# An encoder trunk on one core: waits for single input tiles, banded attention ahead of its gates, and another order of the output stages

## The chip, the cores and the metric

The kernel runs on one core of one Trainium2 chip. The metric is the device time of one execution in microseconds (us), as the median of several runs. Five engines matter: TensorE (PE; the loading of its stationary operand is listed as PEld), VectorE (DVE), ScalarE (ACT), GpSimd (POOL) and SyncE (SP). SP issues all the transfers here, in one queue, in order. Each engine executes its own instructions in the order of the program and waits on semaphores.

## What is computed

Two requests (2048 and 512 tokens, 1024 wide, float32) go through two layers with the same weights:

```python
# layer 0, even
q,k,v,z,gd | qb,kb,vb,zb = split(x @ w_in_even)
ya = gla(q, k, v, log_sigmoid(gd @ w_up + b) / 16)   # gated linear attention, both directions, 4 heads
ya = rms_norm(ya) * norm_g * silu(z)
yb = softmax(qb kb^T + bias, |i-j| <= 128, sink) vb * silu(zb)   # banded attention, 8 heads, 2 kv heads
x  = layer_norm(alpha * x + concat(ya, yb) @ w_out_even)
# layer 1, odd
bg,cg,h,z = split(x @ w_in_odd)
x  = layer_norm(alpha * x + (silu(z) * bg * conv3(cg * h)) @ w_out_odd)
```

Each product is made of three matmuls on pairs of tiles (a high part, rounded, and a low part, the rest): high by high, high by low, low by high.

## The kernel before

The 2560 tokens are cut into five groups of 512; group 4 is the short sequence. The dense work runs in stages, listed in `stages` in `run` (line 1954):

- `e1` (line 955): the input projection of a group. `dense_tok` first makes the token-major part (values and the down-projected gate; two halves of 336 columns, four weights each, for four tiles of 128 tokens), then 21 blocks `u` of 128 channels by 512 tokens with `dense_ch`, 24 matmuls each: 0 to 7 keys and queries of the linear attention, 8 to 12 keys and queries of the banded attention, 13 to 16 the linear attention's gates, 17 to 20 the banded attention's. With `u` 2 to 9 goes a decay matmul each, whose weight `up` is loaded again for each group into one of the large tiles ("y").
- `oe` and `oo` (`out_ln`, line 1614): the output projections, 192 matmuls of 512 columns for a group, added to a residual, then LayerNorm (`norms`, `norm`: two statistics of 512 columns, mean and variance in `mv`, two small ScalarE steps on `mv`, two products 1024 wide, one store).
- `one`: the input projection of the odd layer for group 4, eight blocks of channels, transposed inputs from `prep_odd`.
- `pair` (`odd_pair`, line 1803): the same for two groups of the long sequence at once, with seven block products in place of eight (sums of quarters of weights and inputs). It runs 16 half units of 7 blocks of 12 matmuls. `prep_pair` (line 845) makes the inputs: a first part with transposes, and behind the gate `late` a second one, casts (ScalarE) and low parts (VectorE). `pair_weights` loads two raw weights for each half unit into the weight tiles or free large tiles, forms sums, casts high parts (ScalarE) and makes low parts (GpSimd).

`prep` (line 741) loads the eight input tiles of a stage and makes their high and low parts ("st"). It marks the stage's key when all eight are done, and the stage begins with a wait for that key.

The order of each engine's instructions is written by a planner in Python when the program is built. `Model` keeps a clock for each engine and prices each instruction; a tile counts as one thing in it. `Flow.run` takes the dense work step by step, and `pump` puts in steps of side work, lowest rank first, if VectorE and ScalarE are not too far ahead of TensorE. `until(key)`, at each wait of the dense work, steps side work until the key is marked. Side work is the preparations, residuals, norms (rank 0, `first`), the linear attention (rank 1) and the banded attention (rank 2: `swa_front` makes the probabilities, at most two blocks ahead of `swa_back`, which multiplies by values and gates). All of this orders instructions; on the chip the engines wait for the data itself.

Banded attention starts on a chunk when `done_e1_g` of its groups is marked, that is when all 21 blocks are stored. In `e1`, if the last LayerNorm is not through, the dense work waits for it before `up` is loaded. Large tiles are four "y" tiles and, behind the attention, "tA", "QQ", "KK" and "Q": eight of 128 x 1024.

Weights go from `ws` (two tiles, loaded) to `wh` (three, cast by ScalarE) and `wl` (two, subtracted on GpSimd).

Of the kernel before, what the change touches and what calls it, by code (L numbers as in the profile page):

```python
# [96 lines left out]
class Model:  # L97
# [79 lines left out]

    def note(self, engine, op, outs, ins):
        c = self.clock
        at = c[engine]  # L180
        for x in outs + ins:
            n = x.tensor.name
            w, by = self.written.get(n, (0.0, ""))
            if by != engine:
                at = max(at, w)
            at = max(at, self.free.get(n, 0.0))
        for x in outs:
            at = max(at, self.used.get(x.tensor.name, 0.0) if self.by.get(x.tensor.name) != engine else 0.0)
# [15 lines left out]
        for x in outs:  # L204
            self.fresh.discard(x.tensor.name)
            if x.tensor.name not in self.dram:
                self.written[x.tensor.name] = (end, engine)
        for x in ins:
            if x.tensor.name not in self.dram:
                self.used[x.tensor.name] = max(end, self.used.get(x.tensor.name, 0.0))  # L210
                self.by[x.tensor.name] = engine
# [148 lines left out]
class Trunk:  # L360
    def __init__(self, tc, nc, I, y_out, ctx):
# [37 lines left out]
        self.kept = {}  # L399
# [120 lines left out]
    def dense_ch(self, xh, xl):  # L520

        nc = self.nc
        wh, wl = self.weight()
# [6 lines left out]
        self.drop(wh)  # L530
        self.cook()
# [5 lines left out]
        self.drop(wl)  # L537
        return p

    def dense_tok(self, n, tiles, put):  # L540
# [3 lines left out]
        for kc in range(4):  # L544
            wh, wl = self.weight()
# [195 lines left out]
    def prep(self, key, src, gates, homes=None, hold=False, then=None, fix=None, deep=1):  # L741
# [13 lines left out]
        def get():  # L755
            while todo and self.model.place(homes) and (not raws or eager or (
# [6 lines left out]
        get()  # L763
        yield then
        for k in range(8):
            get()
# [4 lines left out]
            if k % 4 == 0:  # L771
                tiles = [self.st(hold) for _ in range(2)]
                for x, t in zip((hi, lo), tiles):
                    x += [t[:, i] for i in range(4)]
                own += tiles if hold else []
# [10 lines left out]
            def low(h=h, l=l, r=r):  # L786
                nc.vector.tensor_tensor(l, r[:], h.bitcast(F32), op=ALU.subtract)
                self.drop(r)
            if deep > 1:
# [8 lines left out]
        self.flow.mark(key)  # L798

    def prep_odd(self, g, gates):  # L800
# [22 lines left out]
        for hf, t in jobs:  # L823
            get()
            yield raws[:1]
            if t == 0:
                for x in hi, lo:
# [17 lines left out]
    def prep_pair(self, p, gates, late):  # L845
# [78 lines left out]
        for n in (5, 2, 4, 3):  # L924
            hi[n] = self.big_cells() if n != 3 else self.cells(4)
            lo[n] = self.big_cells() if n in (5, 2) else self.cells(4) if n == 4 else []
            for k in range(4):
# [5 lines left out]
                def low(h=h, l=l, r=r):  # L933
                    sub(nc.vector, l, at(r), h.bitcast(F32))
# [9 lines left out]
    def jobs_e1(self):  # L944
        I = self.I
        return ([(I["w_tok"][i, kc].rearrange("p k c -> p (k c)"), 672) for i in range(2) for kc in range(4)]
                + [(I["w_ch"][u].rearrange("p k c -> p (k c)"), 1024) for u in range(21)])
# [7 lines left out]
    def e1(self, g):  # L955
# [5 lines left out]
        cs = slice(4 * g, 4 * g + 4)  # L961
        tiles = [((lambda k, t=t: fh(k)[:, t * 128:t * 128 + 128]), (lambda k, t=t: fl(k)[:, t * 128:t * 128 + 128]))
                 for t in range(4)]
        gd = self.sm((128, 4, 32), "gd")
        stores = {"gla_in": 24, "done_e1_": 37}

        def left(what):
            for key in ("gla_in", "done_e1_") if what == "gla_in" else (what,):
                stores[key] -= 1
                if not stores[key]:  # L970
                    flow.mark("%s%d" % (key, g), max(0.0, self.model.clock["sync"] - flow.t) + 4.5)

# [23 lines left out]
        yield from self.dense_tok(336, tiles, put_v)  # L996
        early = not self.normed or self.normed in flow.done
        if early and g < 4:
            self.load_up()
        yield from self.dense_tok(336, tiles, put_r)  # L1000
        if not early:
            yield self.normed
            self.load_up()
        elif g == 4:
            yield "up"
        up = self.up
        G = None

        def decay(d, h):
            flow.force(G)  # L1010
            p = self.pd()
            nc.tensor.matmul(p[:], up[:, d, h * 128:h * 128 + 128], G[:], start=True, stop=True)
            o = self.m2()
            def rest():
                nc.scalar.activation(o[:], o[:], AF.Exp, scale=1.0 / 16.0)
                flow.defer(lambda: (nc.sync.dma_start(
                    self.d_s[cs, :, d, h * 128:h * 128 + 128].rearrange("c p t -> p c t"),
                    o[:].rearrange("p (c t) -> p c t", c=4)), left("gla_in")), o)
            self.log_sig(p[:], o[:], o, rest)

        def put(dst, h, o):
            flow.defer(lambda: (nc.sync.dma_start(dst[cs, :, h * 128:h * 128 + 128].rearrange("c p t -> p c t"),
                                                  o[:].rearrange("p (c t) -> p c t", c=4)), left("gla_in")), o)

        for u in range(21):
            if u == 14:
                flow.mark("late_" + key)
            p = yield from self.dense_ch(fh, fl)
            if u < 8:
                o = self.m2()  # L1030
                if u < 4:
                    nc.scalar.copy(o[:], p[:])
                    put(self.k_s, u, o)
                else:
                    nc.scalar.activation(o[:], p[:], AF.Copy, scale=128.0 ** -0.5)
                    put(self.q_s, u - 4, o)
                if u == 0:
                    pg = self.pd()
                    for t in range(4):
                        nc.tensor.transpose(pg[:32, t * 128:t * 128 + 128], gd[:, t], self.ident[:])  # L1040
                    G = self.new(self.yp, (128, 512), F32R, "y", 4, True)
                    nc.scalar.copy(G[0:32], pg[:32])
                    nc.scalar.copy(G[64:96], pg[:32])
                    nc.scalar.copy(G[96:128], self.one[96:128].broadcast_to([32, 512]))
# [1007 lines left out]
```

## Time and profile before

| | |
|---|---|
| runs, us | 2436.81, 2434.41, 2434.58 (median 2434.58) |
| profiled execution, us | 2432.03, its span 2430.2 |
| PE busy | 2364.9 us (97%) |
| DVE, ACT, POOL busy | 68%, 50%, 59% |
| mean granted clock of TensorE | 0.992 |
| bytes moved by DMA | 437.33 MB |

The busy time of PE is that of overlapping instructions joined; a single matmul of 512 columns is listed with some 390 ns while the next starts 225 ns after it. In a timeline row the number in brackets is the idle time of that engine just before, and what ended it. The granted clock is a share of 2.4 GHz: 0.5 is 1.2 GHz, and a value between is a mix of the two over the stretch.

The stages in the trace, by the loads of their weights: e1 of group 4 from 6 us, of 3 from about 165, of 2 from about 365, of 1 from about 600; oe4 from about 825; e1 of group 0 from 888; one from about 1100; oe0 from 1378; oe1; oo4; the first pair from 1528; oe2 from about 1843; oe3; oo0; the second pair from 1977; oo1 to oo3 from about 2295 on.

### The profile page before, as it was taken

What the parts mean: (1) busy time and instruction counts of PE and PEld (TensorE: products, weight loads), DVE (VectorE), ACT (ScalarE), POOL (GpSimd) and SP (SyncE); (2) the same over time, 40 slices, a digit from 0 to 9 for tenths busy, and PEclk for the clock granted to TensorE, in tenths of its full rate; (3) what the DMA queues carried; (4) which work ended last, traced back from release to release, by engine and by line L of the source; (5) the groups of instructions that cost most, each with busy time, mean ns of one, the idle gap of its engine ahead of it and who ended that gap; (6) DMA issues with size and microseconds to landing.
All of it is one profiled execution on the core that took longest, in us unless ns stands there. A gap on an engine that the chain in (4) does not pass through costs nothing.

```text
span 2430.2 us, 43123 instructions
## 1 busy us (share of the span) xinstructions
PE 2364.9 (97%) x15830; PEld 1960.5 (81%) x15830; DVE 1653.5 (68%) x2831; ACT 1214.9 (50%) x2336; POOL 1439.6 (59%) x1610
## 2 busy tenths in 40 slices
PE   8999998999999998999999999999999999999998
PEld 7878887778887887877888878788888878888886
DVE  2266766778767887577877566975655788666566
ACT  4565674656565544755566553443334343433431
POOL 5554434445434444354434456898886779989774
PEclk9999999999999999999999999999999999999999
DMA  7967766775766556664566886231225642212473
GB/s 228 284 205 241 222 220 207 217 216 162 254 217 215 171 174 224 196 203 157 183 200 200 267 289 217 84 130 58 73 83 192 220 150 102 79 55 76 150 239 139
DMA packets 273474, 437.33 MB, mean 180 GB/s; under 512 B 21312, under 2 KB 158272, under 8 KB 273264
## 3 DMA queue, kind: packets, MB, share of 16 engines
q1 hardware_dynamic: 273264, 434.59, 55.4%
q8 instruction: 125, 2.05, 0.3%
q14 instruction: 85, 0.70, 0.1%
HBM read 319.67 MB, written 114.84 MB: 179 GB/s over the span
## 4 chain that ended last, share of the span: by engine, by line
PE 65%; DVE 6%; DMA 3%; POOL 2%; ACT 2%; issue 1%; SPq 1%; POOLq 0%; DVEq 0%; ACTq 0%
PE acc L225 55%; PE ps L225 11%; POOL wl L225 1%; DVE QQ L225 1%; DVE st L225 1%; DVE KK L225 1%; DVE P L225 1%; DMA ws<-in_w_oe 1%; SPq L225 1%; DVE y L225 1%; DMA tA<-qf_s 1%; DMA pr<-in_xT 0%; ACT wh L225 0%; DVE ptl L225 0%; DVE md L225 0%
## 5 line engine op out<-in xcount | busy, mean ns | idle before, releaser
L225 POOL TENSOR_TENSOR wl<-ws,wh 128x256 fp32r<-128x256 f32 (+1 forms) x1012 | 833.8, 855 | 807.5 <-PE acc L225 437.3
L225 PE MATMUL acc<-st,wh 128*128 128x512 f32 x3112 | 824.3, 397 | 9.9 <-ACT wh L225 8.8
L225 PEld LDWEIGHTS acc<-st,wh 128*128 128x128 f32 x3112 | 573.2, 189 | 125.6 <-ACT wh L225 11.8
L225 PE MATMUL acc<-st,wl 128*128 128x512 f32 x1720 | 466.2, 396 | 1.7 <-DVE pr L225 1.7
L225 PE MATMUL acc<-wh,st 128*128 128x512 f32 (+1 forms) x1696 | 396.9, 372 | 13.7 <-ACT wh L225 7.4
L225 ACT CAST wh<-ws 128x1024 fp32r<-128x1024 f32 (+2 forms) x277 | 268.0, 968 | 257.9 <-DMA ws<-in_w_ch 63.0
L225 PEld LDWEIGHTS acc<-st,wl 128*128 128x128 f32 x1720 | 317.0, 188 | 64.9 <-issue 2.5
L225 PEld LDWEIGHTS acc<-wh,st 128*128 128x128 f32 x1696 | 303.6, 190 | 62.4 <-ACT wh L225 8.6
L225 PE MATMUL acc<-wl,st 128*128 128x512 f32 (+1 forms) x848 | 212.7, 370 | 1.9 <-POOL wl L225 1.7
L225 ACT ACTIVATE md<-md 128x512 f32<-128x512 f32 x264 | 165.4, 631 | 19.3 <-DVE md L225 13.7
L225 PEld LDWEIGHTS acc<-wl,st 128*128 128x128 f32 x848 | 153.1, 189 | 26.0 <-POOL wl L225 3.2
L225 DVE TENSOR_TENSOR st<-pr,st 128x512 fp32r<-128x512 f32 x115 | 97.9, 865 | 50.7 <-ACT st L225 50.6
L225 DVE SCALAR_TENSOR_TENSOR md<-acc,md 128x512 f32<-128x512 f32 (+1 forms) x110 | 74.5, 683 | 83.7 <-ACT md L225 78.8
L225 POOL TENSOR_TENSOR wh<-md,wh 128x256 fp32r<-128x256 f32 x126 | 102.8, 839 | 16.5 <-ACT wh L225 16.5
L225 ACT CAST pth<-ps 128x512 fp32r<-128x512 f32 x112 | 65.0, 581 | 75.2 <-PE ps L225 72.2
L225 DVE CUSTOM_DVE_ANT_0 P<-ps,P 128x384 f32<-128x384 f32 (+1 forms) x160 | 79.1, 525 | 34.1 <-PE ps L225 33.2
L225 ACT ACTIVATE md<-acc 128x512 f32<-128x512 f32 (+1 forms) x130 | 75.2, 594 | 51.0 <-PE acc L225 50.1
L225 ACT CAST st<-pr 128x512 fp32r<-128x512 f32 x115 | 69.6, 618 | 53.1 <-DMA pr<-in_xT 22.2
L225 ACT ACTIVATE P<-P,nm 128x384 f32<-128x384 f32 (+1 forms) x160 | 93.2, 587 | 3.7 <-DVE nm L225 3.7
L225 ACT COPY km<-KK 128x512 f32<-128x512 f32 x80 | 50.8, 635 | 85.3 <-DVE KK L225 60.0
L225 ACT ACTIVATE mv<-mv,eps 128x1 f32<-128x1 f32 x40 | 11.8, 294 | 153.2 <-DVE mv L225 153.2
L225 ACT CAST wh<-md 128x512 fp32r<-128x512 f32 x63 | 38.8, 620 | 96.0 <-DVE md L225 42.0
(491 smaller groups left out, 4137.9 us busy)
## 6 DMA issues: line engine op xcount, KB each, us to landing
ws<-in_w_ch SPq DMA_DIRECT2D x105, 512.0 KB, 4.3
ws<-in_w_od SPq DMA_DIRECT2D x54, 512.0 KB, 3.9
ws<-in_w_oe SPq DMA_DIRECT2D x40, 512.0 KB, 4.2
ws<-in_w_oo SPq DMA_DIRECT2D x36, 512.0 KB, 3.9
ws<-in_w_tok SPq DMA_DIRECT2D x40, 336.0 KB, 3.2
K<-kb_s SPq DMA_DIRECT2D x32, 384.0 KB, 6.1
y<-in_w_od SPq DMA_DIRECT2D x21, 512.0 KB, 5.1
d_s<-md SPq DMA_DIRECT2D x40, 256.0 KB, 4.4
```

The source lines that it names most:

```text
L225: r = f(*a, **k)
```

## The change

- A stage no longer waits in the plan for all its input tiles: `prep` marks its key at the second of eight tiles and one key for each tile, and `dense_tok` waits for the two tiles of each step. `Model.note` follows the input tiles in parts of 512 columns. `prep` holds its tiles and takes new ones only when two are free. With `each`, a preparation takes tiles one by one as the stage before stores them (od4).
- `e1` is cut into `e1_tok` and `e1_ch`, and the order of the blocks becomes 0 to 12, 17 to 19, 20, 13 to 16. Banded attention's first half waits for a new mark behind block 12 (`swa_in`), its second half for the banded gates (`done_sw`).
- `up` is loaded when the second of the last norm's four rows is done.
- The order of the output stages becomes one, oe0, oo4, oe1, oe2, pair 0, oe3, oo0, pair 1, oo1, oo2, oo3.
- The norms of x1_2 and y_0 get the last rank in place of the first.
- In the second part of `prep_pair` a low part goes to GpSimd in two halves if the planner has GpSimd 1.5 us ahead of VectorE.
- At the end, the first half's statistics are taken before the last matmuls, and the products and the store are made in halves.
- The LayerNorm constants of the odd layer are loaded behind x1_0 in place of x1_1.

```diff
@@ Model
+    def parts(self, x):
+        n = x.tensor.name
+        if not n.startswith("st_"):
+            return (n,)
+        a = x.offset % 2048
+        b = a + sum(s * (m - 1) for s, m in list(x.ap)[1:])
+        return tuple((n, i) for i in range(a // 512, b // 512 + 1))
@@ dense_tok
         for kc in range(4):
+            for k in (2 * kc, 2 * kc + 1):
+                if "%s_k%d" % (key, k) not in self.flow.done:
+                    yield "%s_k%d" % (key, k)
@@ prep
+            if each:
+                yield "%s_%d" % (each, k)
...
+                while self.model.spare("st", 8) < 2:
+                    yield 0.3
+                tiles = [self.st(True) for _ in range(2)]
...
+                self.flow.mark("%s_k%d" % (key, k))
+                if k == 1:
+                    self.flow.mark(key)
...
-        self.flow.mark(key)
@@ prep_pair
-                    sub(nc.vector, l, at(r), h.bitcast(F32))
+                    c = self.model.clock
+                    if c["gpsimd"] + 1.5 < c["vector"]:
+                        for o in (slice(0, 256), slice(256, 512)):
+                            sub(nc.gpsimd, l[:, o], at(r)[:, o], h[:, o].bitcast(F32))
+                    else:
+                        sub(nc.vector, l, at(r), h.bitcast(F32))
@@ e1, now e1_tok and e1_ch
-        stores = {"gla_in": 24, "done_e1_": 37}
+        stores = {"gla_in": 24, "swa_in": 29, "done_sw": 33, "done_e1_": 37}
...
-        if not early:
-            yield self.normed
-            self.load_up()
+                if self.normed:
+                    yield self.normed + "_row1"
+                self.load_up()
@@ swa_front
-        ready = lambda c: all("done_e1_%d" % (x // 4) in done for x in range(c - 1 + self.span(c)[0], c - 1 + self.span(c)[1]))
+        ready = lambda c: all("swa_in%d" % (x // 4) in done for x in range(c - 1 + self.span(c)[0], c - 1 + self.span(c)[1]))
@@ swa_back
             if kv == 0:
+                yield "done_sw%d" % (c // 4)
                 V, gb, o = load(c)
@@ norm
+        parts = (slice(0, 512), slice(512, 1024)) if end else (slice(0, 1024),)
+        for c in parts:
+            nc.vector.scalar_tensor_tensor(y[:, c], y[:, c], mv[:, 0:1], g[:, c], op0=ALU.subtract, op1=ALU.mult)
+            nc.vector.scalar_tensor_tensor(y[:, c], y[:, c], mv[:, 1:2], b[:, c], op0=ALU.mult, op1=ALU.add)
+        if end:
+            for c in parts:
+                nc.sync.dma_start(dst[r * 128:r * 128 + 128, c], y[:, c])
@@ norms
-        if key in ("x1_1", "y_4", "x1_3"):
+        if key in ("x1_0", "y_4", "x1_3"):
@@ out_ln
-            self.flow.add(self.norms(ys, rows, dst, key), 0.0, True)
+            self.flow.add(self.norms(ys, rows, dst, key), 0.0, key not in ("x1_2", "y_0"))
...
+            nc.vector.bn_stats(st[:, 0], ys[i][:, :512])
@@ run
-        stages = [("e1", 4), ("e1", 3), ("e1", 2), ("e1", 1), ("oe", 4), ("e1", 0), ("one", range(8)), ("oe", 0),
-                  ("oe", 1), ("oo", 4), ("pair", 0), ("oe", 2), ("oe", 3), ("oo", 0), ("pair", 1),
-                  ("oo", 1), ("oo", 2), ("oo", 3)]
+        A, B = [*range(13), 17, 18, 19], [20, 13, 14, 15, 16]
+        stages = [("tok", 4), ("ch", ((4,), A + B)), ("tok", 3), ("ch", ((3,), A + B)),
+                  ("tok", 2), ("ch", ((2,), A + B)), ("tok", 1), ("ch", ((1,), A + B)), ("oe", 4),
+                  ("tok", 0), ("ch", ((0,), A + B)), ("one", range(8)), ("oe", 0), ("oo", 4), ("oe", 1), ("oe", 2), ("pair", 0),
+                  ("oe", 3), ("oo", 0), ("pair", 1), ("oo", 1), ("oo", 2), ("oo", 3)]
```

## Rows read from the trace of the kernel before

**Rows 1.** The page's busy times of the whole span: engine, us (share of the span) x instructions.

```profile
PE 2364.9 (97%) x15830; PEld 1960.5 (81%) x15830; DVE 1653.5 (68%) x2831; ACT 1214.9 (50%) x2336; POOL 1439.6 (59%) x1610
```

**Rows 2.** Busy time by stretch of the span: from:to and length in us, then for each engine busy us (x instructions), the granted clock, the DMA share and GB/s.

```profile
0.00:40.00 40.00, 32.96 (x190) 30.55 (x191) 12.88 (x23) 15.79 (x26) 21.87 (x38) 1.00 0.70 226
360.00:400.00 40.00, 35.83 (x270) 33.33 (x269) 21.96 (x42) 23.96 (x66) 16.75 (x27) 0.91 0.71 213
...
920.00:960.00 40.00, 31.36 (x253) 25.62 (x252) 26.67 (x57) 18.04 (x38) 16.05 (x20) 0.91 0.80 270
1520.00:1560.00 40.00, 35.18 (x148) 28.34 (x147) 37.20 (x43) 18.61 (x37) 33.89 (x31) 0.96 0.21 79
1560.00:1600.00 40.00, 40.00 (x178) 33.14 (x177) 37.48 (x43) 15.23 (x26) 39.92 (x35) 1.00 0.42 145
1640.00:1680.00 40.00, 40.00 (x178) 33.13 (x177) 25.00 (x30) 15.19 (x22) 34.55 (x37) 1.00 0.20 66
...
2400.00:2430.20 30.20, 21.67 (x96) 17.62 (x94) 19.86 (x27) 1.99 (x8) 0.01 (x1) 0.90 0.21 87
```

**Rows 3.** For whom TensorE waited in the whole span: us in total, times, longest us.

```profile
PE acc L225 <- ACT wh L225: 16.2, 7, 4.2
...
PE acc L225 <- ACT st L225: 6.1, 1, 6.1
```

**Rows 4.** Timeline of TensorE at the start of the first pair stage: start, us, engine, line, operation, count, and in brackets the idle time before it.

```profile
1528.17 2.88 PE L225 MATMUL acc<-st,wh 128*128 128x512 f32 x12
...
1535.43 1.07 PE L225 MATMUL acc<-st,wl 128*128 128x512 f32 x4
...
1540.41 4.50 PE L225 MATMUL acc<-st,wh 128*128 128x512 f32 x12 [3.91 <-ACT wh L225]
...
1553.99 2.98 PE L225 MATMUL acc<-st,wl 128*128 128x512 f32 x12 [0.91 <-DVE pr L225]
```

**Rows 5.** Timeline of the other engines in the same place.

```profile
1528.98 5.97 DVE L225 TENSOR_TENSOR st<-st 128x512 fp32r<-128x512 f32 x4
...
1537.28 1.27 DVE L225 BATCH_NORM_STATS2 bst<-tA 128x6 f32<-128x512 f32 x2
...
1538.84 0.29 ACT L225 ACTIVATE mv<-mv,eps 128x1 f32<-128x1 f32 x1 [3.23 <-DVE mv L225]
...
1539.27 0.57 ACT L225 COPY pr<-acc 128x512 f32<-128x512 f32 x1
1539.74 0.62 ACT L225 CAST wh<-md 128x512 fp32r<-128x512 f32 x1
...
1540.43 1.88 POOL L225 TENSOR_TENSOR wh<-md,wh 128x256 fp32r<-128x256 f32 x2 [6.03 <-ACT wh L225]
...
1549.12 1.85 DVE L225 SCALAR_TENSOR_TENSOR tA<-tA,mv,ln_g 128x1024 f32<-128x1024 f32 x1
```

**Rows 6.** Timeline of TensorE at the start of the second pair stage.

```profile
1989.77 4.62 PE L225 MATMUL acc<-st,wh 128*128 128x512 f32 x12 [3.92 <-ACT wh L225]
...
2003.35 3.00 PE L225 MATMUL acc<-st,wl 128*128 128x512 f32 x12 [0.78 <-DVE pr L225]
```

**Rows 7.** Groups of VectorE's instructions in the whole span, each shape apart: tiles, shapes, count, then busy us and mean ns of one, then the idle time before them. The tile "ps" lies in PSUM, "st" in SBUF.

```profile
L225 DVE TENSOR_TENSOR st<-st 128x512 fp32r<-128x512 f32 x8 | 12.0, 1552 | 0.0
...
L225 DVE TENSOR_TENSOR st<-ps,st 128x512 fp32r<-128x512 f32 x16 | 10.9, 683 | 0.9 <-ACT st L225 0.9
```

**Rows 8.** The page's costliest group of GpSimd, with the same columns.

```profile
L225 POOL TENSOR_TENSOR wl<-ws,wh 128x256 fp32r<-128x256 f32 (+1 forms) x1012 | 833.8, 855 | 807.5 <-PE acc L225 437.3
```

**Rows 9.** Timeline of VectorE and SP behind the last matmul.

```profile
2422.31 1.28 DVE L225 BATCH_NORM_STATS2 bst<-y 128x6 f32<-128x512 f32 x2
...
2425.26 1.28 DVE L225 SCALAR_TENSOR_TENSOR y<-y,mv,ln_b 128x1024 f32<-128x1024 f32 x1
2426.57 0.33 SPq L225 DMA_DIRECT2D out_y<-y  x1
```

**Rows 10.** Timeline of SP's queue in e1 of group 0: start and us of the issue, transfer.

```profile
907.59 0.32 SPq L225 DMA_DIRECT2D x_s<-y  x1
...
910.47 0.43 SPq L225 DMA_DIRECT2D V<-vb_s  x1
920.38 0.32 SPq L225 DMA_DIRECT2D gb<-gb_s  x1
...
922.51 1.39 SPq L225 DMA_DIRECT2D ws<-in_w_ch  x2
...
935.32 0.42 SPq L225 DMA_DIRECT2D y<-up_s  x1
```

**Rows 11.** Timeline of TensorE in the same place.

```profile
932.03 0.66 PE L225 MATMUL ps<-ident,P 128*128 128x128 f32 x4 [4.50 <-ACT A L225]
...
936.10 0.76 PE L225 MATMUL ps<-v,A 128*128 128x128 f32 x2 [2.20 <-issue]
```

**Rows 12.** Timeline of TensorE in oe1, beside the forward recurrence of the linear attention.

```profile
1433.32 1.21 PE L225 MATMUL ps<-ident,km 128*128 128x128 f32 x4 [1.49 <-ACT km L225]
```

**Rows 13.** Timeline of SP's queue in the first pair stage: stores of the norm's rows and loads of raw weights into large tiles.

```profile
1562.01 0.34 SPq L225 DMA_DIRECT2D out_y<-KK  x1
...
1581.76 0.38 SPq L225 DMA_DIRECT2D KK<-in_w_od  x1
```

**Rows 14.** The page's DMA issues: transfer, count, KB each, median us from issue to landing.

```profile
ws<-in_w_od SPq DMA_DIRECT2D x54, 512.0 KB, 3.9
```

More of the change, by code (lines that the diff above doesn't have):

```diff
@@ L536, in dense_ch, with dense_tok @@
                 yield
[L537 removed]
+        if last:
+            self.drop(wl)
         return p
[L540 removed]
+    def dense_tok(self, n, tiles, put, key):
         nc = self.nc
@@ L739, in let_go, with prep @@
                 self.drop(t)
-    def prep(self, key, src, gates, homes=None, hold=False, then=None, fix=None, deep=1):
+    def prep(self, key, src, gates, homes=None, then=None, fix=None, deep=1, each=None):
         nc = self.nc
@@ L755, in get @@
         def get():
-            while todo and self.model.place(homes) and (not raws or eager or (
+            while todo and (not each or "%s_%d" % (each, todo[0]) in self.flow.done) and self.model.place(homes) and (
+                    not raws or eager or (
                     len(raws) < 6 and self.free_at(homes) <= self.flow.t and (
@@ L771, in prep @@
             if k % 4 == 0:
-                tiles = [self.st(hold) for _ in range(2)]
+                while self.model.spare("st", 8) < 2:
+                    yield 0.3
+                tiles = [self.st(True) for _ in range(2)]
                 for x, t in zip((hi, lo), tiles):
                     x += [t[:, i] for i in range(4)]
-                own += tiles if hold else []
+                own += tiles
             if fix:
@@ L1536, in swa_back, with norm @@
         self.flow.mark("swa_all")
-    def norm(self, y, r, dst, key=None, keep=False):
+    def norm(self, y, r, dst, key=None, keep=False, one=None, st=None):
         nc = self.nc
         g, b = self.ln
-        st = self.sm((128, 2, 6), "bst")
-        for hf in range(2):
+        end = st is not None
+        st = st if end else self.sm((128, 2, 6), "bst")
+        for hf in range(end, 2):
             nc.vector.bn_stats(st[:, hf], y[:, hf * 512:hf * 512 + 512])
@@ L1631, in first @@
             half(0, i, p)
-        yield from self.dense_tok(512, tiles, first)
+        yield from self.dense_tok(512, tiles, first, stage)
         if not end:
-            yield from self.dense_tok(512, tiles, lambda i, p: half(1, i, p))
+            yield from self.dense_tok(512, tiles, lambda i, p: half(1, i, p), stage)
             self.release(stage)
@@ L2013, in run @@
             before, h = stages[n - 1]
-            gate = late[before] % (h[-1] if before == "one" else h)
+            gate = late.get(before, "%s") % (h[-1] if before == "one" else h[0][0] if before == "ch" else h)
             if what == "oe":
```

225 lines of the change are left out of this document (123 added, 102 removed).

## The prediction

> **What bounds the kernel now.** I read the busy times first. TensorE is busy 2364.9 us of a span of 2430.2 [rows 1], so it is idle for 65.3 us in all, and no other engine comes near. The change takes no matmul away and adds none, so it can win only idle time of TensorE, time that TensorE spends at a lower granted clock behind an idle stretch, and the tail. I then cut the span into 40 us windows to see where that time lies [rows 2]. A window inside a pair stage (1640 to 1680) holds 178 matmuls in 40.00 us, 0.2247 us each, with nothing idle: those stages have nothing to give. The first window loses 7.04 us to the start and the last stretch 8.53 to the tail. Of the other 50 us the window from 920 loses 8.64, the one from 360 loses 4.17 and the one from 1520 loses 4.82, and in each of these the granted clock is below 1: part of the window ran at 1.2 GHz instead of 2.4. I then asked for whom TensorE waits [rows 3]: the largest entry is the high part of a weight, which ScalarE casts, 16.2 us in 7 waits. The wait for a high input tile, 6.1 us, is the single one at the start. Last I read the timeline at each loss.
>
> **The pair stages.** At the start of the first pair stage TensorE ends the second block's matmuls at 1536.50 and starts the next at 1540.41, 3.91 idle, waiting for a weight's high part [rows 4]. ScalarE casts that weight at 1539.74. Ahead of it in ScalarE's order stands the LayerNorm's step on mv at 1538.84, which had waited 3.23 for VectorE, and VectorE computes mv's statistics (1537.28) only behind its low parts, four of which took 5.97 [rows 5]. The norm is that of the stage before, y_4, planned in the first rank. The second pair stage repeats it: 3.92 idle, then a wait of 0.78 [rows 6]. The change puts another stage ahead of each pair in time (oe2 for oo4 ahead of the first), and gives the norms that now run there, x1_2 and y_0, the last rank. Then what is late next is the copy of the first block's result (0.57) and the cast (0.62) behind the block's end at 1536.50, some 1.3 us to the matmul. So 2.6 of the 3.9 go. The block behind the wait takes 4.50 where the same 12 matmuls take 2.88 [rows 4]: 1.6 us lost at 1.2 GHz, which I count as won, since the idle time ahead of it is cut to a third. The later waits of 0.91 and 0.78 are for VectorE, which is then in the norm's 1.85 us product [rows 4 to 6]; they go too. That is 2 x (2.6 + 1.6) + 0.9 + 0.8 = 10.1, with bounds of 0 (another wait stands in its place) and 12.8 (all of it).
>
> The norms come later, beside the pair's blocks. Each row is two statistics and two wide products on VectorE and two small steps on ScalarE. VectorE has 15 us free in 40 by 1640 [rows 2], so this is hidden, but each small step can again hold up a cast, and the four large tiles stay taken for longer. Nothing in the trace shows norms there. I charge 2.0, between 0 and what the rival below gives.
>
> In the pair's late preparation a low part may also go to GpSimd when the planner has it 1.5 us ahead. GpSimd was idle for the 6.03 us ahead of 1540.43 [rows 5], just when VectorE was late. A low part costs VectorE 1.55 between two SBUF tiles [rows 7] and GpSimd two halves of 0.86 [rows 8]. I count one part for each pair, with half a microsecond of it on the path: 1.0 in all, between -2 (GpSimd is at 39.92 of 40 from 1560 on [rows 2], so it may owe the time later) and 3.1. VectorE's own price shows what the two engines do to each other: 1.552 us between SBUF tiles, 0.683 with one input in PSUM [rows 7]. The Trainium skill (GPSIMD Engine Reference, 1. Specifications) says that GpSimd shares its SBUF interfaces with VectorE and that they contend when the VectorE instruction has two SBUF inputs; the trace agrees, 1552 against 683 ns. By that rule a part handed over slows the parts that stay, the term is 0 and not 1.0, and the sum below is 13.9 and not 14.9.
>
> **The tail.** Behind the last matmul VectorE adds the residual, takes two statistics in 1.28 and makes two products of 1.28, and the store is issued at 2426.57; the span ends 3.6 later [rows 9]. The change takes the first half's statistics ahead of the matmuls (0.64 gone) and cuts products and store in halves, so that the last store carries half the bytes. Between 0 and 1.8 (half of 3.6) is won on it; a store has a part that does not shrink, so I take 0.7. Sum 1.3.
>
> **The short sequence's gates.** In e1_0 the dense work waited until all of x1_4 was normed, and only then was the decay weight up loaded, at 935.32. Row 2's store was issued at 907.59 [rows 10]. Now two rows are enough, so the planner can put the first channel block earlier. TensorE was idle 4.50 and 2.20 there [rows 11], at a granted clock of 0.91 over the window, that is some 18% of 40 us at 1.2 GHz, worth at most 3.6. But the weights were late as well: the load for in_w_ch stood on SP's queue behind one for gb that went at 920.38, after ten microseconds in which SP issued nothing [rows 10]. The change does not mend that. And the load of up now stands earlier on SP, ahead of weight loads, and waits for a norm's store. Bounds -5 to 9; I take 3.0, nearer to the lower middle because of the weights.
>
> **The order of the output stages.** With oo4 between oe0 and oe1 the forward recurrence has some 43 us more (192 matmuls of 0.2247 us) before its second group is wanted. The wait it covers is 1.49 at 1433 [rows 12]. I take 1.5, bounds 0 to 3.
>
> **What I put at nothing.** Starting a stage with two of its eight tiles: TensorE waits for no input tile after the first [rows 3], since attention work fills the places. Were that cover gone, a start could cost what the longest wait for a weight costs, 4.2 [rows 3]; as a gain it is no more. Banded attention from its own keys and queries, eight blocks (24 x 8 x 0.2247 = 43 us) earlier in each group: TensorE is full while it runs, so this moves work and saves none, except where it fills a hole, which is the first rival. Its second half now waits in the plan for its gates; that holds up two probability tiles, and its V and gate loads go later on SP. The residual loads start with four blocks (22 us) left instead of seven, which covers four loads. Nothing else adds an instruction of note.
>
> **The sum.** 10.1 - 2.0 + 1.0 + 1.3 + 3.0 + 1.5 = 14.9. The profiled execution took 2432.03, 1.83 more than its span; the median of the runs, 2434.58, is 2.55 above it. I take the sum off the median: 2419.7.
>
> **The rivals.** First, more is won: banded work that is ready earlier also fills the starts of the e1 stages. The windows from 360 and 920 lose 12.8 us and up to 7 more at 1.2 GHz [rows 2]; filling two thirds of that beyond the 3.0 counted gives 10 to 12 more, 2408. For it: both losses are in-order waits for weights with little else queued. Against: TensorE's order is fixed in the plan, and work that the plan puts elsewhere doesn't fill a hole that the plan didn't foresee. Second, the stall is only moved: the pair's start waits for the low parts themselves, which were 5.97 us of the backlog [rows 5], or the norms return it; then the pair terms and the gates give nothing and the tail remains, 2433. Third, slower: the large tiles. The weights of the third half unit were loaded at 1581.76 into a tile whose norm had stored it at 1562.01 [rows 13]. With the norms in the last rank, and VectorE at 37.48 of 40 until 1600 [rows 2], four of eight large tiles stay taken. A half unit is 84 matmuls, 18.9 us, and needs two fresh raw weights; with two places only, each waits for landing (3.9 [rows 14]), a cast (0.62) and GpSimd's two halves, together near 8. Two such half units in each pair are 4 x 8 = 32, against the 14.9: 2452. It decides if fewer than two of the four rows are stored 30 us after the pair begins.
>
> **How the numbers follow.** About 0.2% (4.9 us) is what a measurement of this kernel can tell from no change. Forecast 0.56, first rival 0.16, second 0.15, third 0.13. The forecast ends faster by over 0.2% nine times in ten (0.51 and 0.05 the same), the first rival always, the second rival is the same in 0.11, faster in 0.03 and slower in 0.01, the third slower in 0.12 and the same in 0.01. Together: faster 0.70, same 0.17, slower 0.13. The forecast alone spans 2410 to 2430; the range reaches to the first rival below and into the third above, 2402 to 2443.
>
> **What would show it.** Right: no wait of some 3.9 us for a weight at either pair's start, the mv steps of x1_2 and y_0 tens of microseconds into the pair; two stores of half a row at the end; up loaded before the last x1_4 row is stored. Wrong: a wait there for VectorE's low parts (second rival); weight loads in the first 60 us of a pair that wait on SP for a norm's tile (third); new holes above 5 us at the e1 starts, which nothing in this sum foresees.

## The result, and the profile after

| | before | after |
|---|---|---|
| runs, us | 2436.81, 2434.41, 2434.58, 2434.73 | 2417.28, 2411.44, 2404.53, 2415.99 |
| median, us | 2434.65 | 2413.72 |
| profiled execution (span), us | 2432.03 (2430.2) | 2417.28 (2415.5) |

The prediction took the median of the first three runs before, 2434.58. The changed kernel takes 0.9906 of the time before (ratio of the means), 95% interval 0.9877 to 0.9936. Its runs lie 13 us apart, those before 2.4, and the profiled execution is its slowest. A second set on another chip (run 11 below) gave a median of 2414.97 and a ratio of 0.9927 (0.9913 to 0.9940).

The page's first line, against [rows 1]:

```profile
PE 2361.7 (98%) x15830; PEld 1959.9 (81%) x15830; DVE 1643.7 (68%) x2834; ACT 1215.9 (50%) x2336; POOL 1439.3 (60%) x1624
```

The span is 14.7 us shorter: TensorE idles 53.8 us in place of 65.3, and its busy time fell by 3.2. To find the place I cut both spans at the first matmul of each stage. Before: the token part of e1 of group 0, its channel part with one, then oe0 to oo4, the first pair, the second pair, oo1 to the end.

```profile
887.61:932.70 45.09, 38.78 (x371) 35.94 (x370) 38.40 (x73) 15.04 (x38) 26.09 (x31) 1.00 0.54 178
932.70:1378.49 445.79, 434.94 (x3292) 357.34 (x3293) 325.38 (x684) 273.87 (x623) 186.62 (x224) 0.99 0.63 202
1378.49:1528.17 149.68, 147.59 (x701) 122.39 (x700) 93.91 (x132) 65.49 (x152) 92.71 (x106) 0.99 0.74 251
1528.17:1839.69 311.52, 306.70 (x1345) 253.19 (x1344) 217.20 (x260) 123.72 (x190) 271.52 (x273) 0.99 0.25 83
...
1977.53:2290.57 313.04, 307.36 (x1345) 253.07 (x1344) 225.69 (x267) 123.14 (x189) 269.58 (x273) 0.99 0.24 80
2290.57:2430.20 139.63, 131.04 (x577) 107.81 (x575) 88.51 (x109) 42.62 (x72) 86.43 (x91) 0.98 0.56 191
```

After, the same stages; the third row now holds four output stages, oe2 among them.

```profile
898.97:943.06 44.09, 40.37 (x395) 38.38 (x394) 32.23 (x59) 15.32 (x34) 24.36 (x33) 0.92 0.57 184
943.06:1372.04 428.98, 421.62 (x3086) 346.84 (x3085) 299.23 (x642) 268.60 (x626) 179.27 (x221) 1.00 0.65 209
1372.04:1557.12 185.08, 184.66 (x859) 153.48 (x858) 115.06 (x150) 71.10 (x135) 125.11 (x138) 1.00 0.74 249
1557.12:1868.43 311.31, 307.41 (x1345) 253.08 (x1344) 215.55 (x258) 123.53 (x190) 276.09 (x279) 0.99 0.23 79
1962.91:2275.62 312.71, 307.07 (x1345) 252.88 (x1344) 221.56 (x264) 123.31 (x189) 276.25 (x280) 0.99 0.24 79
2275.62:2415.50 139.88, 131.32 (x577) 107.74 (x575) 89.42 (x116) 42.30 (x72) 82.36 (x91) 0.98 0.55 193
```

The pair stages, where the prediction looked for 9.1 us net, are 0.2 and 0.3 us shorter; the stretch of the tail is 0.25 longer. Nearly everything comes ahead of the first pair: it began at 1528.17 and now at 1557.12, and less the 43.1 us of oe2 that now stand ahead of it (192 matmuls of 0.2247) that is 1514.0, or 14.2 earlier. (Run 11's own profile has the pair at 1552.83, so some 4 us of this differ from execution to execution.) Channel part and one take 16.8 less, the output stages 7.7 less, and the stages up to 943 take 10.4 more; part of that is attention work that now stands earlier.

At the pairs one wait has taken the place of another. TensorE now waits for GpSimd's low part "wh" of a weight, and behind the first wait 12 matmuls run in 4.50 us as before [rows 4]:

```profile
1569.10 0.73 PE L237 MATMUL acc<-st,wh 128*128 128x512 f32 x2 [1.84 <-POOL wh L237]
...
1570.81 4.50 PE L237 MATMUL acc<-st,wl 128*128 128x512 f32 x12
```

```profile
1976.67 0.77 PE L237 MATMUL acc<-st,wh 128*128 128x512 f32 x2 [3.62 <-POOL wh L237]
```

GpSimd and ScalarE in the first of these places. GpSimd first makes input low parts, two halves of 1.17 us at a time, and comes to the weight at 1567.88. The norm's step on mv comes at 1572.80, behind the wait, not ahead of the cast as in [rows 5].

```profile
1561.61 2.33 POOL L237 TENSOR_TENSOR st<-ptl,st 128x256 fp32r<-128x256 f32 x2
...
1563.91 2.33 POOL L237 TENSOR_TENSOR qn<-ptl,st 128x256 fp32r<-128x256 f32 x2
...
1567.88 2.30 POOL L237 TENSOR_TENSOR wh<-md,wh 128x256 fp32r<-128x256 f32 x2
...
1572.80 0.29 ACT L237 ACTIVATE mv<-mv,eps 128x1 f32<-128x1 f32 x1 [5.36 <-DVE mv L237]
```

The tail has the form that was expected: the last statistics are of one half, the products and stores are halves.

```profile
2408.58 0.69 DVE L237 BATCH_NORM_STATS2 bst<-Q 128x6 f32<-128x512 f32 x1
...
2411.18 1.78 SPq L237 DMA_DIRECT2D out_y<-Q  x2
```

### The profile page after: what moved, and what is told of

It is laid out like the page before. It is cut to its first block, busy times and chain, and to the rows that moved or that the text cites. A ratio compares the mean times of both kernels' runs of the same rounds, so it can differ in the third digit from the quotient of the medians.

```text
span 2415.5 us, 43163 instructions
## 1 busy us (share of the span) xinstructions
PE 2361.7 (98%) x15830; PEld 1959.9 (81%) x15830; DVE 1643.7 (68%) x2834; ACT 1215.9 (50%) x2336; POOL 1439.3 (60%) x1624
## 4 chain that ended last, share of the span: by engine, by line
PE 77%; DVE 11%; DMA 5%; POOL 3%; issue 2%; ACT 2%; SPq 1%; POOLq 0%; DVEq 0%; ACTq 0%
PE acc L237 62%; PE ps L237 15%; DVE KK L237 2%; POOL wl L237 1%; DVE QQ L237 1%; DMA ws<-in_w_tok 1%; DVE y L237 1%; DVE P L237 1%; DVE st L237 1%; DVE bst L237 1%; SPq L237 1%; DMA pr<-in_xT 1%; POOL wh L237 1%; DVE md L237 1%; DVE Q L237 1%
## 5 line engine op out<-in xcount | busy, mean ns | idle before, releaser
L237 POOL TENSOR_TENSOR wl<-ws,wh 128x256 fp32r<-128x256 f32 (+1 forms) x1012 | 821.7, 843 | 794.1 <-PE acc L237 432.8
L237 PE MATMUL acc<-wh,st 128*128 128x512 f32 (+1 forms) x1632 | 382.1, 373 | 12.5 <-ACT st L237 5.8
L237 PEld LDWEIGHTS acc<-wh,st 128*128 128x128 f32 x1632 | 293.9, 191 | 60.4 <-ACT wh L237 6.2
L237 PE MATMUL acc<-wl,st 128*128 128x512 f32 (+1 forms) x816 | 204.6, 371 | 2.0 <-POOL wl L237 1.9
L237 PEld LDWEIGHTS acc<-wl,st 128*128 128x128 f32 x816 | 146.8, 189 | 25.1 <-POOL wl L237 2.9
L237 ACT CAST pth<-ps 128x512 fp32r<-128x512 f32 x112 | 65.3, 583 | 77.2 <-PE ps L237 69.9
L237 DVE TENSOR_TENSOR ptl<-ps,pth 128x512 fp32r<-128x512 f32 x112 | 76.2, 681 | 17.6 <-ACT pth L237 17.4
```

The source lines that it names most:

```text
L237: r = f(*a, **k)
```

## The experiments

Ratios stand against the kernel before on the same chip. Runs 1 to 4, 5 to 8 and 9 to 12 shared a chip each.

| run | median, us | ratio (95%) |
|---|---|---|
| 1 norms first | 2418.67 | 0.9946 (0.9930 to 0.9962) |
| 2 norms first, low parts on VectorE | 2411.99 | 0.9916 (0.9901 to 0.9931) |
| 3 fewer low parts on GpSimd | 2409.82 | 0.9909 (0.9895 to 0.9924) |
| 4 old gates | 2423.74 | 0.9962 (0.9948 to 0.9976) |
| 5 kernel before, new gates | 2433.77 | 1.0003 (0.9991 to 1.0014) |
| 6 stages wait for all tiles | 2413.61 | 0.9915 (0.9897 to 0.9934) |
| 7 old order | 2419.04 | 0.9936 (0.9915 to 0.9956) |
| 8 up waits for whole norm | 2415.70 | 0.9925 (0.9903 to 0.9948) |
| 9 decay at its old place | 2427.89 | 0.9977 (0.9968 to 0.9987) |
| 10 kernel before, decay moved | 2397.38 | 0.9853 (0.9839 to 0.9866) |
| 11 changed kernel again | 2414.97 | 0.9927 (0.9913 to 0.9940) |
| 12 as run 3 | 2406.61 | 0.9888 (0.9873 to 0.9903) |

**The pair stages: runs 1, 2, 3, 11 and 12.** Theory A was that the late norms win their time at the pairs, theory B that the low parts which VectorE and GpSimd share bound the pair starts. Run 1 puts the norms of x1_2 and y_0 into the first rank again, run 2 also keeps all low parts on VectorE, run 3 gives GpSimd fewer, run 11 is the changed kernel again and run 12 is run 3 again, both on one chip.

```diff
@@ runs 1 and 2
-            self.flow.add(self.norms(ys, rows, dst, key), 0.0, key not in ("x1_2", "y_0"))
+            self.flow.add(self.norms(ys, rows, dst, key), 0.0, True)
@@ run 2
-                    if c["gpsimd"] + 1.5 < c["vector"]:
+                    if False:
@@ runs 3 and 12
-                    if c["gpsimd"] + 1.5 < c["vector"]:
+                    if c["gpsimd"] + 3.5 < c["vector"]:
```

> The kernel after, but the norms of x1_2 and y_0 get the first rank again, as every norm had before; TensorE's order up to the first pair stage stays as it is after. Theory A (the prediction's): the norm's small step on ScalarE is what held the weight casts at the pair starts, so the waits for a high part come back and the pair stages, 311.3 and 312.7 us after, grow by 3 to 5 us each; the time rises by 5 to 9 us. Theory B: the pair starts are bound by the low parts that VectorE and GpSimd share, and the norm only stood where the wait was seen; each pair stage stays within 1.5 us and the time within 3 us of the kernel after.

> The kernel after, with the norms of x1_2 and y_0 in the first rank and all low parts of the pair preparation on VectorE: both edits at the pair starts undone, all else of the change kept. Theory A: the pair stages are slower than after by some 5 us each (10 in all), TensorE waiting 3.9 us for a high part as before. Theory B: they come out at the 311.5 and 313.0 us that they took before, that is within 1 us of after, and the whole time within 3 us of after, so that none of the change's gain comes from the pair starts.

> The kernel after, but a low part goes to GpSimd only if the planner has it 3.5 us ahead of VectorE in place of 1.5, so that fewer go there. Theory A (GpSimd's help is worth half a microsecond a pair): the pair stages get up to 2 us longer. Theory B (GpSimd's input parts delay its weight parts, on which TensorE waits 1.84 and 3.62 us at the two pair starts after): those waits shrink and the pair stages get 1 to 3 us shorter each, unless VectorE's low parts take the wait over, in which case they stay within 1 us.

> The changed kernel once more, for its spread and as the partner of the next kernel on the same chip: 2411 to 2417 by every theory.

> The changed kernel with the bound for GpSimd's low parts at 3.5 us in place of 1.5, beside the changed kernel on the same chip. Theory H: the low parts on GpSimd lengthen each pair stage by some 3 us, since they hold up the low parts of the weights, so this kernel is 4 to 8 us below the changed kernel, its pair stages 308 to 309.5. Theory A (the prediction, low parts on GpSimd worth 0.5 us a stage): 1 us above it, the pair stages as long as the changed kernel's, 311 to 313.

The two pair stages took 310.92 and 313.04 us in run 2 and 311.42 and 312.13 in run 11. In run 1 and in run 3:

```profile
1553.21:1867.02 313.81, 307.55 (x1345) 253.38 (x1344) 213.46 (x256) 124.45 (x190) 277.39 (x282) 0.99 0.23 78
1961.10:2279.09 317.99, 310.73 (x1345) 255.07 (x1344) 221.09 (x264) 124.18 (x189) 274.62 (x281) 0.98 0.23 78
```

```profile
1555.71:1863.77 308.06, 306.13 (x1345) 251.79 (x1344) 212.26 (x257) 123.32 (x190) 274.12 (x275) 1.00 0.24 80
1957.92:2267.30 309.38, 305.82 (x1346) 251.98 (x1345) 223.78 (x267) 123.33 (x189) 271.31 (x275) 1.00 0.24 80
```

In run 12:

```profile
1554.28:1862.37 308.09, 306.14 (x1345) 251.74 (x1344) 212.57 (x257) 123.35 (x190) 274.36 (x275) 1.00 0.23 80
...
1958.16:2268.32 310.16, 307.37 (x1346) 253.12 (x1344) 223.89 (x267) 123.24 (x189) 268.83 (x275) 0.99 0.24 80
```

So GpSimd's low parts cost 2.9 and 5.0 us with early norms (run 1 against 2), and 3.2 and 2.6 with late ones (changed kernel against run 12; 3.3 and 2.0 with run 11 in its place). The late norms win 2.9 and 3.7 (run 2 against 3, which still has a few parts on GpSimd) and 2.5 and 5.3 (run 1 against the changed kernel; 2.4 and 5.9 with run 11). These are lengths from one profile each; the two profiles of the changed kernel differ by 0.1 and 0.6. Run 1 came out as theory A expected, run 2 as theory B. The changed kernel has both effects, and they cancel: with both edits undone (run 2) the pairs are as long as in the kernel before. By medians run 12 is 8.4 us below run 11 on one chip, and the intervals do not overlap; for the late norms alone the whole time shows less, 2.2 between runs 2 and 3, with intervals that overlap. Late norms with no low part on GpSimd at all were not run.

The durations show why the hand-over loses. Low parts of the same shape in the changed kernel (count, then shortest, median and longest in ns, first and last start): VectorE, then GpSimd.

```profile
L237 DVE TENSOR_TENSOR st<-K,st x1: 1226/1226/1226, 1561.0 to 1561.0; 128x512 fp32r<-128x512 f32 x1
```

```profile
L237 POOL TENSOR_TENSOR st<-K,st x2: 1182/1182/1183, 1559.3 to 1560.5; 128x256 fp32r<-128x256 f32 x2
```

In run 3:

```profile
L237 DVE TENSOR_TENSOR st<-K,st x1: 679/679/679, 1559.7 to 1559.7; 128x512 fp32r<-128x512 f32 x1
```

```profile
L237 POOL TENSOR_TENSOR ptl<-qn,st x2: 742/966/1190, 1964.8 to 1965.5; 128x256 fp32r<-128x256 f32 x2
```

The same subtraction takes VectorE 679 ns while GpSimd stands still and 1226 beside it, and a half takes GpSimd 742 or 1190. The 1552 ns of [rows 7] was no price of two SBUF inputs by themselves. The trace of before could have told this: the four slow ones of [rows 5] ran beside GpSimd, the two behind them while it stood still.

```profile
1529.26 1.75 POOL L225 TENSOR_TENSOR md<-ws,md 128x512 f32<-128x512 f32 x1
1530.96 1.74 POOL L225 TENSOR_TENSOR tB<-y 128x512 f32<-128x512 f32 x1
1532.78 1.62 POOL L225 TENSOR_TENSOR A<-tB,Q 128x512 f32<-128x512 f32 x1
...
1534.88 1.28 DVE L225 TENSOR_TENSOR st<-K,st 128x512 fp32r<-128x512 f32 x2
```

**Single tiles, the decay weight and the order: runs 6, 7 and 8.** Each undoes one edit of the changed kernel. Run 6 puts back only the wait for all eight tiles, not the way tiles are held. Run 7 also moves the preparations to fit its order and makes the norms of y_4 and y_0 the late ones, and in it the rows of oe1 are scaled with the odd layer's constants, which the change loads behind x1_0.

```diff
@@ run 6
-                if k == 1:
+                if k == 7:
                     self.flow.mark(key)
...
-                if "%s_k%d" % (key, k) not in self.flow.done:
+                if False:
@@ run 7
-                  ... ("oe", 0), ("oo", 4), ("oe", 1), ("oe", 2), ("pair", 0),
+                  ... ("oe", 0), ("oe", 1), ("oo", 4), ("pair", 0), ("oe", 2),
@@ run 8
-                    yield self.normed + "_row1"
+                    yield self.normed
```

> The changed kernel, in which a stage waits in the plan for all eight input tiles again. Theory A (the prediction): a stage's inputs are ready ahead of it, so the single-tile waits are worth nothing: 2412 to 2416. Theory C: part of the gain came from stage starts (the idle time at e1 of groups 2 and 1 fell with them), so 2417 to 2421 and longer idle time of TensorE at the first matmuls of e1 of groups 2, 1 and 0.

> The changed kernel with the output stages in the old order (one, oe0, oe1, oo4, pair 0, oe2, ...), its late norms being those of oo4 and oo0. Theory A (the prediction): the order is worth 1.5 us, the wait for the forward recurrence in oe1, so 2415 to 2417. Theory D: the stage that now stands ahead of the pair covers its preparation, and most of the 7.7 us by which the four stages ahead of the first pair got shorter comes from it, so 2419 to 2422 and idle time of TensorE again between oe0 and the first pair.

> The changed kernel, in which the load of the decay weight waits for the whole norm of oe4 again. Theory A (the prediction): the wait for row 1 in place of row 3 is worth 3.0 us, so 2416 to 2418. Theory E: in the changed kernel the decay weight's load still comes late (issued at 940.89, 8 us behind the weights at 932.87) and TensorE still idles 3.6 us before it, so the edit brings nothing: 2412 to 2416.

Run 6 cannot be told from the changed kernel: no worth of single tiles can be seen. Run 8 is 2.1 above run 6, and their intervals overlap: no gain from up can be seen, though 3.0 is too little to be ruled out by the times. Run 7 is 5.4 above run 6, but the intervals overlap. Its profile (span 2412.6, its fastest run) puts the first pair at 1508.60, where run 11 has 1509.7 less oe2, and 7.9 us of idle time between the channel part and the pair, where the changed kernel has 7.8: the traces show no gain from the order. Between 0 and 5 us is as far as this goes.

**The gates: runs 4 and 5.** Run 4 takes the gates out of the changed kernel, run 5 puts them into the kernel before. In run 5 the weights keep their old order, so that each branch gets the other's gates; its instructions are the same in kind and number.

```diff
@@ run 5, on the kernel before
-        for u in range(21):
-            if u == 14:
+        for u in [*range(13), 17, 18, 19, 20, 13, 14, 15, 16]:
+            if u == 20:
...
-        ready = lambda c: all("done_e1_%d" ...
+        ready = lambda c: all("swa_in%d" ...
@@ run 4
-        A, B = [*range(13), 17, 18, 19], [20, 13, 14, 15, 16]
+        A, B = [*range(13)], [13, 14, 15, 16, 17, 18, 19, 20]
...
-        ready = lambda c: all("swa_in%d" ...
+        ready = lambda c: all("done_e1_%d" ...
```

> The kernel after, but the blocks of the channel part run in the old order 0 to 20 and the banded attention waits again for all of them; all else of the change kept. Theory C (banded work that is ready earlier fills holes of the e1 stages and leaves less behind the last one): slower than after by 8 to 14 us, with the dense stage between the start of group 0's channel blocks and oe0 growing from 429 us towards 446. Theory D (the gain lies in the order of the output stages, the earlier loading of up or the single tiles): within 4 us of after.

> The kernel before with one edit: blocks in the order 0 to 12, 17 to 20, 13 to 16, and banded attention's first half free behind block 12, its second half behind the banded gates. Theory A (the prediction): the earlier start is worth nothing, the time stays at that of the kernel before, 2432 to 2435. Theory B (from the run in which the changed kernel got the old gates and came to 2423.7 against 2413.7): the banded matmuls move from behind e1 of group 0 into the stages before it and fill TensorE there, about 10 us, so 2423 to 2426; the stretch from the first channel block of group 0 to oe0 (445.8 us before) becomes shorter by 10 to 17 and the first pair stage begins some 10 us earlier.

Without the gates the changed kernel loses some 10 us (0.9962 against 0.9906 and 0.9927), so I took them for the cause; put into the kernel before they bring nothing. Theory B of run 5 fell. In run 5 the stages ahead of the channel part got shorter (it began at 912.24, not 932.70) and the stretch behind got longer:

```profile
912.24:1385.23 472.99, 449.94 (x3601) 368.18 (x3600) 339.17 (x736) 288.97 (x685) 190.33 (x225) 0.97 0.64 206
```

23.05 us of it TensorE idles, and the mean granted clock is 0.97. Its largest waits stand at the end of the stretch, where TensorE's order holds nothing but the linear attention's recurrence:

```profile
1368.11 1.36 PE L225 MATMUL ps<-ident,km 128*128 128x128 f32 x4 [3.65 <-ACT km L225]
...
1377.98 1.35 PE L225 MATMUL ps<-ident,km 128*128 128x128 f32 x4 [6.81 <-ACT km L225]
...
1384.23 1.35 PE L225 MATMUL ps<-ident,km 128*128 128x128 f32 x4 [3.19 <-ACT km L225]
```

**One line that nobody had named: runs 9 and 10.** Beside the gates more differs in e1 than the list of the change and its diff show. One thing is the decay matmul of blocks 8 and 9. Before, it and the three ScalarE steps on its result stood ahead of that block's two evictions (a high and a low part, read from the accumulator), after, behind them. Run 9 undoes only this, run 10 does only this. Two others were not tested by any run: for groups 3 to 1 up was loaded between the two halves of the token part and is now loaded behind both, and the input preparations of groups 2, 1 and 0 and of oe4 now go on only at the end of an earlier group.

```diff
@@ run 10, on the kernel before
-                elif u > 1:
-                    decay((u - 2) // 4, (u - 2) % 4)
             elif u < 13:
-                if u < 10:
-                    decay(1, u - 6)
                 sc = 1.0 if u == 8 else 0.125
...
+            if 1 < u < 10:
+                decay((u - 2) // 4, (u - 2) % 4)
             yield
```

> The changed kernel with one small thing undone that neither the change's list nor the prediction named: the decay matmul of blocks 8 and 9 stands again ahead of the two evictions of its own block, not behind them. Theory F: what counts is how much attention the plan gets placed ahead of the stages one and oe0; the gates do it only together with this, so undoing it costs as much as undoing the gates did: 2422 to 2426, the stretch from group 0's first channel block to oe0 is 450 us or longer in place of 429, and TensorE waits there for the recurrence (tile km). Theory G: the gates alone moved the attention and the place of a decay matmul is worth nothing: 2412 to 2417, that stretch 429.

> The kernel before with that one edit: the decay matmul of blocks 8 and 9 behind the evictions of its block, the gates of banded attention as before. Theory F: attention comes earlier without any change of the gates, the stretch from group 0's first channel block to oe0 falls from 446 to below 440, and the time by 4 to 10 us to 2424 to 2429. Theory G: nothing, 2431 to 2435, that stretch 446.

Run 9 is 12.9 us above run 11, a little more than theory F gave it: all the change's other edits together leave 0.9977. Run 10 is 35.5 below the kernel before and 17.6 below the changed kernel, far more than theory F gave it. Theory G fell in both. Run 9 has the waits of run 5 again. The first row below is the stretch from the channel part to oe0, the second the waits for km in the whole span (us, times, longest), of which 11.4 us lie in that stretch:

```profile
902.89:1370.48 467.59, 448.21 (x3587) 366.16 (x3585) 333.79 (x721) 278.17 (x632) 193.19 (x228) 0.98 0.63 202
```

```profile
PE ps L237 <- ACT km L237: 14.0, 5, 7.2
```

Run 10, the page's first line:

```profile
PE 2355.9 (98%) x15830; PEld 1953.8 (81%) x15830; DVE 1655.7 (69%) x2831; ACT 1218.2 (51%) x2336; POOL 1433.5 (60%) x1610
```

Its span is 2397.6, so TensorE idles 41.7 us in place of 65.3, and the same number of matmuls is busy for 9.0 us less, at a mean granted clock of 0.996 in place of 0.992. The same stages as above (token part, channel part and one, three output stages, first pair):

```profile
880.77:922.88 42.11, 42.11 (x378) 40.29 (x376) 36.12 (x71) 19.16 (x48) 22.09 (x30) 1.00 0.55 181
922.88:1351.02 428.14, 422.61 (x3213) 346.54 (x3212) 311.39 (x656) 268.36 (x610) 185.16 (x223) 1.00 0.64 208
1351.02:1494.53 143.51, 143.04 (x681) 119.11 (x680) 94.94 (x129) 63.42 (x139) 95.44 (x106) 1.00 0.77 253
1494.53:1806.04 311.51, 307.59 (x1346) 253.88 (x1344) 217.50 (x260) 123.66 (x190) 271.82 (x273) 0.99 0.24 83
```

For whom TensorE waits on attention tiles (ps) in the whole span: us, times, longest. Before:

```profile
PE ps L225 <- DVE ptl L225: 6.3, 7, 2.4
...
PE ps L225 <- DVE QQ L225: 5.8, 7, 2.3
PE ps L225 <- ACT A L225: 5.0, 2, 4.5
PE ps L225 <- DVE mx L225: 2.9, 2, 2.7
```

In run 10:

```profile
PE ps L225 <- DVE ptl L225: 2.3, 3, 1.3
PE ps L225 <- ACT A L225: 1.8, 1, 1.8
```

The token part has no idle time at all, and up is loaded there at 926.41 without the change's edit. The pair is as before, with its first wait unmended:

```profile
1506.78 3.78 PE L225 MATMUL acc<-st,wh 128*128 128x512 f32 x8 [3.92 <-ACT wh L225]
```

Seven kernels side by side. "Attention ahead" is TensorE's busy time from 5 us to the first channel block of group 0 on matmuls that write tile ps and read no weight tile (some dense blocks write ps too); idle is TensorE's, up to that block and from there to the first pair; the pair's start is less 43.1 where oe2 stands ahead of it.

| kernel | attention ahead | channel part begins | idle up to it | idle from it | pair begins |
|---|---|---|---|---|---|
| before | 244.9 | 932.7 | 28.2 | 12.9 | 1528.2 |
| run 5 | 237.2 | 912.2 | 17.3 | 23.1 | 1524.9 |
| run 4 | 232.5 | 901.7 | 10.5 | 20.7 | 1521.3 |
| run 9 | 233.9 | 902.9 | 13.8 | 25.0 | 1524.7 |
| after | 260.0 | 943.1 | 22.7 | 7.8 | 1514.0 |
| run 12 | 259.8 | 941.0 | 21.4 | 8.4 | 1511.2 |
| run 10 | 254.6 | 922.9 | 12.4 | 6.0 | 1494.5 |

With 233 to 245 us of attention ahead the idle time behind is 13 to 25, with 255 to 260 it is 6 to 8. Run 10 also has little idle time ahead; the changed kernel pays 10 us more there.

## Why the prediction was right, point by point

The median came 6.0 us below the forecast of 2419.7, and faster was right. But its terms were not where the time came from. Two steps failed and made up for each other: the pairs got 0.5 us shorter in place of 9.1 (10.1 - 2.0 + 1.0), and a line that the sum does not hold gave the rest. That the total came out so near is luck.

- **The pairs, 10.1 - 2.0.** The mechanism was right: with the norm's mv step behind the cast, that wait is gone. By the lengths of the stages the late norms won 6.5 to 8.2 for both pairs, against 8.1. The 3.92 us wait stands unchanged in run 10, which leaves the pairs alone. In the changed kernel itself the 1.6 us at the lower clock was not won back: behind waits of 1.84 and 0.40 the 12 matmuls took 4.50 again.
- **Low parts on GpSimd, +1.0 between -2 and 3.1.** This step failed, in sign and bounds: -5.3 to -7.8 for both pairs (by medians -8.4, run 11 against 12). "One part for each pair" was wrong, the traces show five handed over in the first pair, four of them in GpSimd's order ahead of the weight's low part, for which TensorE then waits. The reason for the lower bound ("GpSimd is at 39.92 of 40") had the right place at too small a price, and for the pairs the second rival came true ("the stall is only moved"), though the wait is for a weight's low part on GpSimd and not for VectorE's. The Trainium skill (GPSIMD Engine Reference, 1. Specifications) says that the two engines contend for shared SBUF interfaces when VectorE reads two SBUF inputs; the trace agrees, 679 against 1226 ns on VectorE and 742 against 1190 on GpSimd. The 0 that the prediction drew from that rule was nearer than its own 1.0, but still too good.
- **The tail, 1.3.** From the last matmul's end to the end of the span 7.68 us in place of 8.53, 0.85: right. But TensorE idles 0.82 at 2341.91 for a norm's step on mv, a wait that runs 11 and 12 have too, and the stages from oo1 on took 139.88 in place of 139.63.
- **up, 3.0.** Mis-read. up did come earlier against the program: issued at 940.89, 2.2 us ahead of the first channel block and ahead of the last norm's store (954.50), where it had been 2.6 behind the block (935.32 against 932.70). But that is still 8 us behind the load of the first weights, and it brought nothing: with the whole norm waited for again (run 8) the first pair begins at 1552.25, in run 11 at 1552.83. The wait of 4.50 [rows 11] was for the attention's tile A, and both waits are gone in run 10, where up's gate is the old one.
- **The order, 1.5.** Between 0 and 5 by the times, nothing in the traces; open.
- **Single tiles, 0.** Run 6 shows nothing else.
- **"Banded attention from its own keys and queries ... saves none."** This is the other step that failed, in part. Its premise, that TensorE is full while attention runs, holds for the early stages only. At the end of one, the recurrence runs with nothing beside it if attention is late there (run 5, 13.7 us in three waits). The first rival looked for such a gain, and it came to 10 to 13 us (runs 4 and 9), but neither from the holes at the e1 starts (up to the channel part the changed kernel idles 22.7 us, run 4 10.5) nor from the gates by themselves (run 5).
- **The third rival's price.** Its parts add to 6.2 (3.9 + 0.62 + 2 x 0.86) and not to "near 8", so its time would have been about 2445, not 2452. It did not come.
- **What was not in the list.** The place of the decay matmul carries the result: undone, 12.9 of 17.9 us of gain are lost (runs 9 and 11); alone, it brings 35.5. The diff in the section on the change leaves it out.

How it acts is only half shown. Runs 9 and 10 show that it decides, and the table shows what goes with it: how much attention the plan places ahead, and how much idle time remains behind. Near blocks 8 and 9 themselves no wait of TensorE was found that could carry 35 us. From the first group on the order of all engines' instructions is another, since each step of the plan depends on the clocks that the steps before have left. Why the moved evictions lead the plan to a better order, and whether that is more than luck of this one plan, stays open. The runs say little on that rival: only 4, 5, 8, 9 and 10 change which attention matmuls stand ahead of the channel part, and of these run 8 is the one other small edit; it left the time where it was. Open too is why the other edits cost 17.6 us beside it: all of that lies ahead of the first pair (1494.5 against 1514.0, or 1509.7 in run 11), 10 us of it as idle time up to the channel part, where the two untested edits act as well; the pairs are as long in both, since there the late norms and GpSimd's low parts cancel.

The fastest kernel run here is that of run 10, the kernel before with the decay moved: 2397.38. With pair stages as long as those of run 12 it would be 6.3 us shorter; that was not run.

## What to carry to other kernels

Where a planner writes the order of the instructions, go through the diff for every line that moves a step, however small: one matmul, moved with the three steps on its result, brought twice what the whole change did, and an edit put into another plan (run 5) was worth nothing. Undo an edit in the new kernel and do it alone in the old one before you call it the cause; the gates passed the first test and failed the second. Work handed to an engine that has idle time lands in its order ahead of what others wait for, and can slow the engine that handed it over.

## What the hardware showed

VectorE's subtraction of 512 columns with both inputs in SBUF took 679 ns with GpSimd quiet and 1226 beside its steps of 256 columns; the eight of [rows 7], most of them beside GpSimd's steps of 512, took 1552 on average. GpSimd's 256 columns took 742 and 1190. An estimate from these durations: both engines together are slower than VectorE alone, since in the 2.36 us in which GpSimd makes one part (two halves of 1.18) VectorE beside it makes 1.9 (2.36 / 1.226), together 2.9; alone it would make 3.5 (2.36 / 0.679).
